# An FFN between pieces: where weight copies stand in the queues, which engine makes low parts and square sums, and where a scale chain keeps its temporary

## The chip, the cores and the metric

One core of one Trainium2 chip. The metric is the device time of one execution in microseconds. Below, PE is TensorE, DVE is VectorE, ACT is ScalarE, POOL is GpSimd, and SP is SyncE, which issues all of the kernel's loads and stores.

## The reference

One step of a hybrid streaming layer in float32: attention heads and gated linear attention heads side by side, their outputs concatenated, then a feed-forward network (FFN). 2048 prompt tokens and 32 sample tokens, model width 1024, FFN width 4096. The change touches only the end of it:

```python
h = x + concat(A, B) @ w_out
y = h + relu(rmsnorm(h) @ w_up)^2 @ w_down
```

## The kernel before

The attention and the linear attention run first (to about 745 us) and leave their concatenated output, the mix, in DRAM. Then `ffn_phase` (L1005) does the rest in three pieces, of two groups of tokens each: 320 columns per group in piece 0, 360 in pieces 1 and 2. Tokens lie along the columns, features along the partitions, in 8 blocks of 128 (KB = 8, H = 4).

Every float32 matrix is kept as a pair of a high part (a rounding copy in fp32r, made by ACT) and a low part (the difference, made by DVE or POOL), and a product is three matmuls: high by high, low by high, high by low.

A piece has these stages. `load_mix` (L955) brings the mix of a group and splits it: ACT copies the high part, DVE subtracts for the low part (L967, L968). `project_out` (L971) multiplies by w_out, giving PSUM tiles `op`, one for each feature block f. `first_group` and `second_group` (L1148, L1153) add the residual, keep y, add up the squares of y for the norm (`square`, L1134) and form the operands of a Strassen-like 2x2 scheme for the up projection: B11 and B21 from the first group, T1, T2 and T4 from combinations of both groups (`diff` L1140, `fused` L1145, `pair` L1118), then T3 and B22 after the loop. Block by block of 256 FFN columns (NF = 16), `up_head`, `up_first` (block 0) and `up_rest` do 7 products of 12 matmuls each (A11, A12, S1, S2, A22, S3, S4 by B11, B21, T1, T2, T4, T3, B22), `finished` (L1199) applies the scale, relu and square and splits u, and `down` (L1241) does 48 matmuls for each group and adds to y.

In block 0 alone `token_sums` (L1052) sums the squares over partitions with matmuls (`ss`), and a chain of 11 small DVE instructions (`rsqrt`, L163: two on the bit pattern, then three rounds of three) makes the scale, which `token_scale` (L1065) spreads with matmuls (`rb`) and ACT copies to `cb`. The order of PE in block 0: A11, A12, S1, S2, ss, A22, S3, rb, S4, down.

Weights: `up_weights` (L1074) loads a block of w_up in two halves and makes its seven operands; 7 high parts on ACT (L1088), 7 low parts (L1089) and 4 combinations (L1091) on POOL. `rows_pair` (L213) with `split_weight` (L185) does the same for w_down, two loads, two ACT copies (L194) and two POOL subtractions (L198) of 1024 columns; `load_wout` (L951) for w_out. Staging tiles come from a pool of 5 that the mix, the temporaries and the weights share; the split weights from a pool of 8. PSUM has a pool of 3 and one of 5 slots.

Two kinds of seam lie between pieces. At an up seam (the last `op` tiles, T2, T4, T3, B22, the scale, block 0) block 0's weights are split, and block 1's after them: L1185 calls `weights` for block 0 in the loop over `op` tiles, when the second group's f = 3 is done; L1283 calls it for block 1 behind `up_first`. At a mix seam (block 15 of one piece, then the next piece's projection) L1285 to L1287 split the next mix and half of w_out.

The order of the work in each engine's queue is not the program's order. A planner simulates the queues at build time and lists each engine's instructions; an instruction on one engine can be tied behind another of the same engine by an edge that costs no semaphore (as PE's are, L89). Each queue then runs strictly in that order. What the change's lines do is quoted in the diff; the central calls before are:

```python
weights = lambda pi, b: (up_weights(b, f"wu{pi}_{b}"), self.rows_pair(w_dn, 2 * b, f"wd{pi}_{b}", engs))
...
if (gi, f) == (1, H - 1):
    with tc.issue_after(self.y_loads if pi == 0 else self.last_load):
        ws[0] = weights(pi, 0)
```

Of the kernel before, what the change touches and what calls it, by code (L numbers as in the profile page):

```python
# [28 lines left out]
class Builder:  # L29
# [155 lines left out]
    def split_weight(self, src, hi, lo, hi_eng="act", lo_eng="pool", parts=1):  # L185
# [14 lines left out]
    def cols_pair(self, w, c0, name, engs=(("act", "pool"), ("act", "pool")), k0=0, nk=KB):  # L200
# [3 lines left out]
        for i in range(2):  # L204
            ks = slice(i * nk // 2, (i + 1) * nk // 2)
            self.split_weight(w[:, k0 + ks.start : k0 + ks.stop, c0 : c0 + n], h[:, ks, :], l[:, ks, :], *engs[i])
        return h, l

    def wide_pairs(self, w, c0, name, engs=(("act", "pool"), ("act", "pool")), parts=range(2)):

        return [self.cols_pair(w, c0, f"{name}{j}", engs, 4 * j, 4) for j in parts]
# [793 lines left out]
    def ffn_phase(self, pieces):  # L1005
# [7 lines left out]
        with ExitStack() as ctx:  # L1013
# [29 lines left out]

            def next_mix(pi, gi):
# [376 lines left out]
```

## Time and profile before

| | us |
|---|---|
| median of 3 runs (2358.19 to 2358.8) | 2358.7 |
| profiled execution, device time | 2357.7 |
| its span, first to last instruction | 2355.9 |
| PE busy | 2271.3 |
| DVE busy | 1452.7 |
| POOL busy | 1163.2 |
| ACT busy | 953.4 |
| mean granted TensorE clock | 0.970 |

The device time of the profiled execution is 1.8 us more than its span. The page gives for each engine the time that its instructions ran; a view of waits tells who let an engine go on after an idle time; a table by stretches gives busy times and the granted clock of any stretch, where 1.00 is 2.4 GHz and 0.50 is 1.2 GHz; a view in order of time shows single instructions. Matmuls are pipelined, so the time of one overlaps the next.

### The profile page before, as it was taken

The page shows a single profiled execution, that of the slowest core. Times are in us where ns is not written, and L with a number is a line of the kernel's source. Part 1 is how long each engine was busy: PE and PEld are TensorE (multiplying, and loading weights), DVE is VectorE, ACT ScalarE, POOL GpSimd, SP SyncE. Part 2 cuts the span into 40 slices and gives each one's busy share as a digit, 9 for nine tenths or more (in the row PEclk, how much of TensorE's full clock was granted, in tenths as well). Part 3 has the DMA queues.
Part 4 walks back from the last instruction along what each step waited for, and adds up shares of the span by engine and source line. Part 5 has one row for each costly group of instructions (what it writes and reads, how often), then busy time and mean ns, then how long its engine had stood idle before and what let it go on. Part 6 is the DMA issues. An engine that isn't in the chain of part 4 may idle for free.

```text
span 2355.9 us, 39800 instructions
## 1 busy us (share of the span) xinstructions
PE 2271.3 (96%) x15389; PEld 2130.4 (90%) x15389; DVE 1452.7 (62%) x3670; ACT 953.4 (40%) x1953; POOL 1163.2 (49%) x956
## 2 busy tenths in 40 slices
PE   6999999899998899999999899999999999999999
PEld 5777776788877899999999899999999999999999
DVE  6765656788886855555554755555555755555555
ACT  3554445454552733333334433333334533333331
POOL 3221224232430567667753466666653546666662
PEclk8999999889988899999999999999999999999999
DMA  8764563322333412222235222222227122222221
GB/s 219 148 127 101 130 166 121 84 75 74 92 93 86 119 57 91 89 72 72 81 112 169 72 72 72 72 72 72 72 62 224 37 80 72 72 72 72 72 63 51
DMA packets 214461, 221.56 MB, mean 94 GB/s; under 512 B 38736, under 2 KB 178976, under 8 KB 214272
## 3 DMA queue, kind: packets, MB, share of 16 engines
q1 hardware_dynamic: 214272, 219.02, 33.2%
q8 instruction: 121, 1.98, 0.4%
q14 instruction: 68, 0.56, 0.1%
HBM read 180.08 MB, written 38.91 MB: 93 GB/s over the span
## 4 chain that ended last, share of the span: by engine, by line
PE 79%; DVE 12%; DMA 3%; ACT 2%; POOL 2%; issue 1%; SPq 0%; DVEq 0%; POOLq 0%; ACTq 0%
PE dn L105 31%; PE op L105 7%; PE PS4B L105 4%; PE PA11B L105 4%; PE PA12B L105 4%; PE PS2T L105 4%; PE PS1T L105 3%; PE PS3T L105 3%; PE PA22T L105 3%; PE zq L105 3%; PE zr L105 3%; DVE AT L881 2%; PE zkv L105 2%; PE zv L105 2%; PE O L105 1%
## 5 line engine op out<-in xcount | busy, mean ns | idle before, releaser
L1089 POOL TENSOR_TENSOR wu<-stage,wu 128x512 fp32r<-128x512 f32 x336 | 435.2, 1304 | 528.1 <-ACT wu L1088 528.0
L1256 DVE TENSOR_TENSOR y<-y,dn 128x360 f32<-128x360 f32 (+1 forms) x768 | 392.4, 514 | 222.2 <-PE dn L105 218.7
L1088 ACT ACTIVATE wu<-stage 128x512 fp32r<-128x512 f32 x336 | 205.9, 627 | 488.8 <-PE dn L105 224.7
L1091 POOL TENSOR_TENSOR stage<-stage 128x512 f32<-128x512 f32 x192 | 250.5, 1305 | 7.5
L1209 ACT ACTIVATE r<-PA11B 128x360 f32<-128x360 f32 (+1 forms) x48 | 22.0, 458 | 317.7 <-PE PA11B L105 317.7
L1196 DVE TENSOR_TENSOR PA12B<-PA12B,r 128x360 f32<-128x360 f32 (+1 forms) x48 | 25.3, 527 | 150.2 <-PE PA12B L105 150.2
L105 PE MATMUL PS2T<-T2h,wu 128*128 128x360 f32 (+1 forms) x384 | 100.6, 324 | 13.3 <-ACT T2h L1121 13.3
L708 POOL TENSOR_TENSOR g<-g,ggla 128x512 f32<-128x512 f32 (+1 forms) x17 | 25.1, 1494 | 171.9 <-ACT g L113 171.9
L105 PE MATMUL PA22T<-T4h,wu 128*128 128x360 f32 (+1 forms) x384 | 103.1, 332 | 0.0
L105 PE MATMUL PS3T<-T3h,wu 128*128 128x360 f32 (+1 forms) x384 | 100.7, 326 | 0.0
L105 PE MATMUL PS4B<-B22h,wu 128*128 128x360 f32 (+1 forms) x384 | 100.4, 325 | 0.0
L105 PE MATMUL PS1T<-T1h,wu 128*128 128x360 f32 (+1 forms) x384 | 98.9, 321 | 0.0
L105 PE MATMUL PA11B<-B11h,wu 128*128 128x360 f32 (+1 forms) x384 | 98.8, 321 | 0.0
L105 PE MATMUL PA12B<-B21h,wu 128*128 128x360 f32 (+1 forms) x384 | 98.7, 321 | 0.0
L881 DVE COPY_PREDICATED AT<-masks,A 64x64 f32<-64x64 int32 (+1 forms) x330 | 82.9, 253 | 13.9 <-PE A L105 4.0
L105 PEld LDWEIGHTS PS2T<-T2h,wu 128*128 128x128 f32 x384 | 68.8, 190 | 14.1 <-ACT T2h L1121 14.1
L805 POOL TENSOR_TENSOR E<-cc 128x256 f32<-128x256 f32 (+1 forms) x117 | 68.2, 617 | 24.9 <-PE A L105 19.7
L497 ACT ACTIVATE P<-S,negm 128x192 f32<-128x192 f32 (+2 forms) x128 | 51.5, 417 | 52.9 <-DVE negm L492 32.8
L105 PEld LDWEIGHTS PA22T<-T4h,wu 128*128 128x128 f32 x384 | 71.4, 197 | 0.0
L105 PEld LDWEIGHTS PS3T<-T3h,wu 128*128 128x128 f32 x384 | 69.9, 193 | 0.0
L105 PEld LDWEIGHTS PS4B<-B22h,wu 128*128 128x128 f32 x384 | 69.1, 191 | 0.0
L105 PEld LDWEIGHTS PS1T<-T1h,wu 128*128 128x128 f32 x384 | 68.1, 188 | 0.0
(1006 smaller groups left out, 7769.3 us busy)
## 6 DMA issues: line engine op xcount, KB each, us to landing
stage<-in_w_up SPq DMA_DIRECT2D x96, 512.0 KB, 3.8
stage<-in_w_down SPq DMA_DIRECT2D x96, 512.0 KB, 3.9
stage<-in_w_out SPq DMA_DIRECT2D x24, 512.0 KB, 4.7
xT1a<-in_xT_prompt SPq DMA_DIRECT2D x16, 512.0 KB, 8.0
stage<-in_w_in SPq DMA_DIRECT2D x16, 512.0 KB, 5.0
x1a<-in_x_prompt SPq DMA_DIRECT2D x16, 512.0 KB, 7.2
out_yT_prompt<-y SPq DMA_DIRECT2D x32, 180.0 KB, 3.8
m<-mixT SPq DMA_DIRECT2D x11, 512.0 KB, 4.7
```

The source lines that it names most:

```text
L105: self._pe(self.T.matmul(out, lhsT, rhs, start=start, stop=stop), ns)
L497: S.activation(Pt[:, u, :n], sp[:, jp], AF.Exp, bias=negm[:, ch, u : u + 1], scale=0.125, accum_out=rsum[:, ch, u : u + 1],)
L708: G.tensor_tensor(out=gv, in0=gv, in1=ggla[:r].unsqueeze(1).broadcast_to([r, 4, P]), op=ALU.mult)
L805: G.tensor_tensor(out=e4, in0=c4, in1=ref, op=ALU.subtract)
L881: V.copy_predicated(dst, mk.unsqueeze(1).broadcast_to([L // nh, 2, w // m, m]), src[r].rearrange("s p (n m) -> s p n m", m=m),)
L1088: S.activation(h, src, AF.Copy)
L1089: G.tensor_tensor(out=l, in0=src, in1=f32(h), op=ALU.subtract)
L1091: tt = lambda o, x, y, op: G.tensor_tensor(out=o, in0=x, in1=y, op=op)
L1196: tt = lambda out, x, y, op=ALU.add: V.tensor_tensor(out=out, in0=x, in1=y, op=op)
L1209: S.activation(r0, product(b, "A11", "B11"), AF.Copy)
L1256: V.tensor_tensor(out=yg[:, f, :], in0=yg[:, f, :], in1=ps, op=ALU.add)
```

## The change

- `rsqrt` can keep its temporary q in PSUM, and does for the scale of the FFN; its first instruction now writes q instead of y.
- Copies that split weights can be tied behind a given instruction of ACT (`after`). Tied are: block 0's down weights behind T4's last high copy, and their call moves from the middle of the loop over `op` tiles to its end; block 1's up and down weights behind T3's last high copy; the next piece's first half of w_out behind the last block's high copy of u number 3.
- The low parts of the next mix are made by POOL instead of DVE.
- For the second group's f = 4, 5 and 6 the squares go to r0 and r1 in SBUF instead of back to the PSUM tile, and POOL adds them to the sum.

```diff
+    def after(self, ins, other):
+        if other is not None:
+            self.tc.add_manual_dep(ins.ins, other.ins.name, NOSYNC, reason="order")
+        return ins
...
-    def rsqrt(self, ms, r, n, name, y=None, q=None):
+    def rsqrt(self, ms, r, n, name, psum=False):
         V = self.V
-        if y is None:
-            y = self.small.tile([P, 16], F32, tag="rsq_y", name=f"rsq_y_{name}")[:r, :n]
+        y = self.small.tile([P, 16], F32, tag="rsq_y", name=f"rsq_y_{name}")[:r, :n]
+        if psum:
+            q = self.ps_s(f"rsq_q_{name}")[:r, :n]
+        else:
             q = self.small.tile([P, 16], F32, tag="rsq_q", name=f"rsq_q_{name}")[:r, :n]
-        yi = y.bitcast(I32)
-        V.tensor_scalar(out=yi, in0=ms.bitcast(I32), scalar1=1, scalar2=None, op0=ALU.logical_shift_right)
-        V.tensor_scalar(out=yi, in0=yi, scalar1=-1, scalar2=0x5F3759DF, op0=ALU.mult, op1=ALU.add)
+        yi, qi = y.bitcast(I32), q.bitcast(I32)
+        V.tensor_scalar(out=qi, in0=ms.bitcast(I32), scalar1=1, scalar2=None, op0=ALU.logical_shift_right)
+        V.tensor_scalar(out=yi, in0=qi, scalar1=-1, scalar2=0x5F3759DF, op0=ALU.mult, op1=ALU.add)
         for _ in range(3):
             V.tensor_tensor(out=q, in0=y, in1=y, op=ALU.mult)
...
             if hi_eng == "act":
-                self.S.activation(hi[:, ks], raw, AF.Copy)
+                self.after(self.S.activation(hi[:, ks], raw, AF.Copy), after)
...
-    def load_mix(self, g, hi, lo):
+    def load_mix(self, g, hi, lo, eng=None):
...
-                self.V.tensor_tensor(out=l[:, :, ts], in0=m[:, ks], in1=h[:, :, ts].bitcast(F32), op=ALU.subtract)
+                (eng or self.V).tensor_tensor(out=l[:, :, ts], in0=m[:, ks], in1=h[:, :, ts].bitcast(F32), op=ALU.subtract)
...
             def next_mix(pi, gi):
-                self.load_mix(pieces[pi][gi], hi, lo)
+                self.load_mix(pieces[pi][gi], hi, lo, G)
...
             def token_sums(name, N, accs):
-                return self.rsqrt(ms, r, 2 * n, f"y{name}")
+                return self.rsqrt(ms, r, 2 * n, f"y{name}", psum=True)
...
                 def square(gi, f, sq):
                     acc, yf = sums[gi], y[gi][:, f, :]
+                    pool = gi == 1 and H <= f < KB - 1
+                    if pool:
+                        sq = r[f % 2]
                     S.activation(sq if f else acc, yf, AF.Square)
                     if f:
-                        V.tensor_tensor(out=acc, in0=acc, in1=sq, op=ALU.add)
+                        (G if pool else V).tensor_tensor(out=acc, in0=acc, in1=sq, op=ALU.add)
...
                         fused(y[0][:, f, :], g(f), ps, ALU.subtract)
-                        pair("T4", k, ps)
+                        end[0], _ = pair("T4", k, ps)
...
                     if (gi, f) == (1, H - 1):
                         with tc.issue_after(self.y_loads if pi == 0 else self.last_load):
-                            ws[0] = weights(pi, 0)
+                            wu = up_weights(0, f"wu{pi}_0")
+                with tc.issue_after(self.y_loads if pi == 0 else self.last_load):
+                    ws[0] = wu, down_weights(pi, 0, end[0])
...
-                    S.activation(uh[i], ps, AF.Copy)
+                    hi = S.activation(uh[i], ps, AF.Copy)
+                    if i == 3:
+                        end[0] = hi
...
-                    pair("T3", k, t)
+                    end[0], _ = pair("T3", k, t)
...
-                        ws[b + 1] = weights(pi, b + 1)
+                        x = end[0] if b == 0 else None
+                        ws[b + 1] = up_weights(b + 1, f"wu{pi}_{b + 1}", x), down_weights(pi, b + 1, x)
...
-                        wo = self.load_wout(pi + 1, (0,))
+                        wo = self.load_wout(pi + 1, (0,), after=end[0])
```

## Rows read from the trace of the kernel before

**Rows 1.** The page, parts 1 and 4: busy time of each engine, and the chain that ended last by engine.

```profile
PE 2271.3 (96%) x15389; PEld 2130.4 (90%) x15389; DVE 1452.7 (62%) x3670; ACT 953.4 (40%) x1953; POOL 1163.2 (49%) x956
...
PE 79%; DVE 12%; DMA 3%; ACT 2%; POOL 2%; issue 1%; SPq 0%; DVEq 0%; POOLq 0%; ACTq 0%
```

**Rows 2.** Waits of PE over the whole span: who waited for whom, us in total, times, the longest.

```profile
PE PS2T L105 <- ACT T2h L1121: 13.3, 3, 5.4
PE dn L105 <- DVE ul L1196: 6.9, 5, 3.4
...
PE rb L105 <- DVE rsq_y_y L175: 4.6, 3, 1.9
...
PE PS2T L105 <- DVE T2l L1123: 4.3, 3, 2.7
```

**Rows 3.** Busy time in eight stretches: length, busy us and instructions of PE, PEld, DVE, ACT and POOL, granted clock, DMA share, GB/s. The first three run from the first product of block 0 to the first of block 1 (up seams of pieces 0, 1 and 2), the next two from the end of the last block's products to the next piece's first output projection (mix seams 1 and 2); then one regular block of 320 and one of 360 columns; last, four microseconds within mix seam 1.

```profile
792.53:834.70 42.17, 31.69 (x167) 30.44 (x165) 33.46 (x58) 19.40 (x42) 26.42 (x17) 0.72 0.37 113
1308.35:1344.76 36.41, 29.23 (x157) 27.72 (x157) 32.52 (x56) 19.00 (x39) 24.20 (x15) 0.86 0.36 116
1862.89:1899.29 36.40, 29.92 (x157) 28.45 (x157) 32.51 (x56) 19.00 (x39) 24.29 (x15) 0.86 0.38 116
1224.26:1244.99 20.73, 16.78 (x98) 15.76 (x97) 17.54 (x35) 7.76 (x17) 5.78 (x3) 0.92 0.63 198
1781.73:1799.54 17.81, 16.17 (x97) 15.71 (x97) 16.36 (x33) 8.94 (x14) 7.21 (x4) 1.00 0.95 319
880.70:907.14 26.44, 26.44 (x182) 26.44 (x182) 14.42 (x31) 9.44 (x19) 18.67 (x14) 1.00 0.26 81
1425.97:1455.63 29.66, 29.66 (x182) 29.66 (x181) 15.83 (x31) 9.79 (x19) 18.66 (x14) 1.00 0.23 71
1229.00:1233.00 4.00, 3.98 (x16) 3.99 (x17) 2.23 (x5) 1.98 (x3) 2.38 (x1) 0.57 0.79 241
```

**Rows 4.** PE in up seam 1, in order of time: start, us, what; in brackets the idle time before it and its releaser.

```profile
1319.89 0.67 PE L105 MATMUL PS2T<-T2h,wu 128*128 128x360 f32 x1 [3.96 <-ACT T2h L1121]
1321.29 0.67 PE L105 MATMUL PS2T<-T2l,wu 128*128 128x360 f32 x1 [0.73 <-DVE T2l L1123]
...
1322.05 2.42 PE L105 MATMUL ss<-ones,sums 128*120 128x1 f32 x12
...
1332.26 1.60 PE L105 MATMUL rb<-packed,rsq_y_y 120*128 120x120 f32 x12 [1.86 <-DVE rsq_y_y L175]
...
1336.90 0.43 PE L105 MATMUL dn<-ul,wd_0h 128*128 128x360 f32 x1 [0.57 <-DVE ul L1196]
```

**Rows 5.** VectorE in up seam 1, in order of time (x2 is two in a row).

```profile
1310.69 3.85 DVE L1125 SCALAR_TENSOR_TENSOR B22l<-y,packed,B22h 128x360 fp32r<-128x360 f32 x2
...
1315.91 1.41 DVE L1143 SCALAR_TENSOR_TENSOR r<-y,packed,r 128x360 f32<-128x360 f32 x1
...
1317.68 1.15 DVE L1125 SCALAR_TENSOR_TENSOR B22l<-y,packed,B22h 128x360 fp32r<-128x360 f32 x1
1318.75 0.58 DVE L1146 SCALAR_TENSOR_TENSOR op<-y,packed,op 128x360 f32<-128x360 f32 x1
...
1324.51 0.16 DVE L1062 TENSOR_SCALAR msy<-ss 120x6 f32<-120x6 f32 x1
...
1327.02 1.19 DVE L173 TENSOR_TENSOR rsq_q_y<-rsq_y_y 120x6 f32<-120x6 f32 x1
...
1331.09 1.11 DVE L175 SCALAR_TENSOR_TENSOR rsq_y_y<-rsq_q_y,rsq_y_y 120x6 f32<-120x6 f32 x1
```

**Rows 6.** Groups of VectorE instructions over the whole span: busy us, mean ns of one.

```profile
L1256 DVE TENSOR_TENSOR y<-y,dn 128x360 f32<-128x360 f32 x512 | 269.0, 528 | 155.3 <-PE dn L105 153.0 <-DMA stage<-in_w_down 0.5
...
L1125 DVE SCALAR_TENSOR_TENSOR B22l<-y,packed,B22h 128x360 fp32r<-128x360 f32 x8 | 11.8, 1499 | 0.7 <-ACT B22h L1121 0.7
...
L1125 DVE SCALAR_TENSOR_TENSOR B21l<-op,packed,B21h 128x360 fp32r<-128x360 f32 x8 | 4.7, 593 | 9.8 <-ACT B21h L1121 9.8
...
L968 DVE TENSOR_TENSOR T4l<-m,T4h 128x512 fp32r<-128x512 f32 x4 | 2.6, 678 | 0.0
```

**Rows 7.** GpSimd in up seam 1, in order of time.

```profile
1307.53 5.07 POOL L198 TENSOR_TENSOR wd_0l<-stage,wd_0h 128x1024 fp32r<-128x1024 f32 x2 [15.63 <-ACT wd_0h L194]
```

**Rows 8.** The page, part 5: the costliest group, GpSimd's low halves of the up weights.

```profile
L1089 POOL TENSOR_TENSOR wu<-stage,wu 128x512 fp32r<-128x512 f32 x336 | 435.2, 1304 | 528.1 <-ACT wu L1088 528.0
```

**Rows 9.** VectorE in up seam 0, in order of time.

```profile
797.86 4.54 DVE L1125 SCALAR_TENSOR_TENSOR B22l<-y,packed,B22h 128x320 fp32r<-128x320 f32 x3
```

**Rows 10.** Mix seam 1, all engines in order of time.

```profile
1222.67 1.67 ACT L967 ACTIVATE T4h<-m 128x128 fp32r<-128x128 f32 x4
...
1222.84 2.40 POOL L198 TENSOR_TENSOR wo_00l<-stage,wo_00h 128x1024 fp32r<-128x1024 f32 x1 [4.84 <-ACT wo_00h L194]
...
1223.00 2.40 DVE L968 TENSOR_TENSOR T4l<-m,T4h 128x128 fp32r<-128x128 f32 x1 [1.03 <-ACT T4h L967]
...
1224.24 0.42 ACT L1203 ACTIVATE PA22T<-PA22T 128x320 f32<-128x320 f32 x1
...
1228.49 0.47 DVE L1196 TENSOR_TENSOR ul<-PA22T,uh 128x320 fp32r<-128x320 f32 x1
...
1229.02 0.41 PE L105 MATMUL dn<-ul,wd_15h 128*128 128x320 f32 x1 [3.42 <-DVE ul L1196]
```

**Rows 11.** PE in mix seam 2.

```profile
1784.69 0.43 PE L105 MATMUL dn<-ul,wd_15h 128*128 128x360 f32 x1 [1.64 <-DVE ul L1196]
```

More of the change, by code (lines that the diff above doesn't have):

```diff
@@ L183, in rms, with split_weight @@
         return self.rsqrt(ss, r, 1, name)
-    def split_weight(self, src, hi, lo, hi_eng="act", lo_eng="pool", parts=1):
+    def split_weight(self, src, hi, lo, hi_eng="act", lo_eng="pool", parts=1, after=None):
         k, c = src.shape[1], src.shape[2]
@@ L205, in cols_pair, with wide_pairs, rows_pair @@
             ks = slice(i * nk // 2, (i + 1) * nk // 2)
-            self.split_weight(w[:, k0 + ks.start : k0 + ks.stop, c0 : c0 + n], h[:, ks, :], l[:, ks, :], *engs[i])
+            self.split_weight(w[:, k0 + ks.start : k0 + ks.stop, c0 : c0 + n], h[:, ks, :], l[:, ks, :], *engs[i], after=after)
         return h, l
-    def wide_pairs(self, w, c0, name, engs=(("act", "pool"), ("act", "pool")), parts=range(2)):
-        return [self.cols_pair(w, c0, f"{name}{j}", engs, 4 * j, 4) for j in parts]
-    def rows_pair(self, w, k0, name, engs=(("act", "pool"), ("act", "pool"))):
+    def wide_pairs(self, w, c0, name, engs=(("act", "pool"), ("act", "pool")), parts=range(2), after=None):
+        return [self.cols_pair(w, c0, f"{name}{j}", engs, 4 * j, 4, after) for j in parts]
+    def rows_pair(self, w, k0, name, engs=(("act", "pool"), ("act", "pool")), after=None):
         h, l = self.w_tile(f"{name}h"), self.w_tile(f"{name}l")
@@ L217, in rows_pair @@
         for i in range(2):
-            self.split_weight(w[:, k0 + i : k0 + i + 1, :], h[:, i : i + 1], l[:, i : i + 1], *engs[i])
+            self.split_weight(w[:, k0 + i : k0 + i + 1, :], h[:, i : i + 1], l[:, i : i + 1], *engs[i], after=after)
         return h, l
@@ L948, in gla_phase, with load_wout @@
                         Q.dma_start(self.o[name][2 * p + hh], St[key][hh * 64 : hh * 64 + 64, p, :])
-    def load_wout(self, pi, halves=range(2), engs=(("act", "pool"), ("act", "pool"))):
+    def load_wout(self, pi, halves=range(2), engs=(("act", "pool"), ("act", "pool")), after=None):
         w_out = self.a["w_out"].rearrange("(k p) n -> p k n", p=P)
-        return [self.wide_pairs(w_out, 512 * fh, f"wo{pi}_{fh}", engs) for fh in halves]
-    def load_mix(self, g, hi, lo):
+        return [self.wide_pairs(w_out, 512 * fh, f"wo{pi}_{fh}", engs, after=after) for fh in halves]
+    def load_mix(self, g, hi, lo, eng=None):
         off = 0
@@ L1042, in load_y @@
                 return yt
+            end = [None]
             def next_mix(pi, gi):
@@ L1072, in token_scale, with up_weights @@
                 S.activation(cb[gi], rb, AF.Copy)
-            def up_weights(b, name):
+            def up_weights(b, name, after=None):
                 raw = []
@@ L1087, in pair @@
                     h, l = ws[x]
-                    S.activation(h, src, AF.Copy)
+                    self.after(S.activation(h, src, AF.Copy), after)
                     G.tensor_tensor(out=l, in0=src, in1=f32(h), op=ALU.subtract)
@@ L1105, in ffn_phase @@
             engs = (("act", "pool"), ("act", "pool"))
-            weights = lambda pi, b: (up_weights(b, f"wu{pi}_{b}"), self.rows_pair(w_dn, 2 * b, f"wd{pi}_{b}", engs))
+            down_weights = lambda pi, b, after=None: self.rows_pair(w_dn, 2 * b, f"wd{pi}_{b}", engs, after)
             mix = list(self.mix)
```

14 lines of the change are left out of this document (8 added, 6 removed).

## The prediction, made before the changed kernel ran

> **What bounds the kernel now.** I read the page first. PE is busy for 96% of the span and carries 79% of the chain that ended last [rows 1], so only time that PE does not use, or uses at the lower clock, can be won. The waits of PE say where it is: its four largest waits add up to 29.1 us, and all four lie in the FFN, at the seams between pieces [rows 2]. The table by stretches prices a seam. A regular block takes 26.44 us at 320 columns and 29.66 us at 360, PE never idle, for 180 matmuls (7 products of 12, two groups of 48 down matmuls) [rows 3]. An up seam holds 132 of them, so 19.39 or 21.75 us, and the sums and broadcasts of the scale. Those two show 2.42 us at half clock and 1.60 [rows 4]; halving the first, I allow 2.8 us (an estimate). The seams take 42.17, 36.41 and 36.40 us [rows 3]: they lose 20.0, 11.9 and 11.9. A mix seam holds 96 down matmuls, 14.1 or 15.8 us; they take 20.73 and 17.81 [rows 3]: lost 6.6 and 2.0. Together 52.4 us, which is all that this change can touch.
>
> Why they lose it. In up seam 1 PE waits 3.96 us for the last high part of T2, 0.73 us for its low part, 1.86 us for the scale chain and 0.57 us for u [rows 4], and runs much of the rest at 1.2 GHz: granted clock 0.86 over the seam, 0.72 in seam 0 [rows 3]. The operands are late because VectorE is: the combination that the last T2 is copied from starts at 1318.75, behind B22's low parts, of which two take 3.85 us and one 1.15, and a difference that takes 1.41 [rows 5]. The groups say what is odd about them: B22l, two SBUF tensors in, takes 1.50 us in the mean; B21l, the same instruction with one input from PSUM, 0.59 [rows 6]. GpSimd's low parts of the down weights run just then, 5.07 us for two [rows 7]. In seam 0 three B22l take 4.54 us [rows 9]. The scale chain shows the same: 0.16 us for the instruction that reads PSUM, 1.19 and 1.11 for two on SBUF alone, 7.7 us from 1324.51 to the end of the last [rows 5]. An instruction with a PSUM input is not held: 512 of them take 528 ns in the mean beside a GpSimd that is busy 63% of a regular block [rows 3, 6].
>
> **The change, part by part.**
>
> *Copies of the down weights behind T4's last copy, of block 1's weights behind T3's.* This takes the 5.07 us of GpSimd and block 1's 1.30 us pieces [rows 7, 8] out of the stretch before the last T2. Four B22l give back 0.9 us each and the difference 0.8: 4.4 us. ACT does no more than before. Down weights are due at the first down matmul, at least three products and the scale's 2.8 us after T4's last copy, some 9 us, against 2 us of copies and 5 of low parts. Block 1's need 11 GpSimd instructions, 14.3 us by rows 8, and they start behind those 5: some 20 us after T4, while its first two pairs are due after about 18 and only the rest after 28. The first pairs come first, so hidden; were the cover gone, each us late is a us of PE. The two SP loads of down weights move past no other load, but hold two of the five staging tiles longer, so the second half of block 1's up weights lands some 9 us later, inside the same slack.
>
> *Three sums of squares to GpSimd.* VectorE loses three instructions of 0.5 us, about one of them ahead of the last T2: 0.5. GpSimd gains three of about 0.92 us (1304 ns x 360/512, rows 8), each of which can hold one two-SBUF instruction of VectorE: 0 to 2.8 us, of which I take 1. ACT writes the squares to r0 and r1; the first product's copy and T3's first difference then wait for GpSimd to have read them, which they need only after a product's 2 us. The last sum, still on VectorE, waits for GpSimd's third; GpSimd has little else there. First stretch: waits of 4.69 less 4.9 plus 1, so 0.8 us left.
>
> *The chain in PSUM.* Of eleven instructions eight now have one tensor input at most in SBUF and a PSUM operand beside or behind it. The three squarings of y still read SBUF twice, with a PSUM output that no row shows. Bounds: 0.17 each, or held by a whole GpSimd instruction, 1.3 to 2.5 us. I take held for 1.25 us each, because the same line was held in rows 5 and its inputs have not moved: 3.8. With twelve steps of 0.2 us and one T3 instruction between them the chain takes 6.7 us instead of 7.7, since the moved weights now lie beside it. At full clock PE has two products, 4.0 us, to cover it: 2.7 us of wait remain. T3's last difference and low part meet the same GpSimd work, and T3's last copy can stand behind 2 us of moved copies on ACT: 0 to 5 us, I take 1.5. The wait for u, 0.6, stays. The temporary takes one of five PSUM slots; the last projection's and PS2T's are free by then, so I cost it at nothing (a product's 2 us if not).
>
> *Clock.* The 3.42 us stall in mix seam 1 was followed by four us at 0.57 [rows 3, 10], a loss of 1.7; the 1.64 us stall of mix seam 2 by none, the stretch shows 1.00 [rows 3, 11]. The waits left lie between, so 0 or 1.7 per up seam; I take 1.7.
>
> Up seams therefore keep 0.8 + 2.7 + 1.5 + 0.6 + 1.7 = 7.3 us each: gains of 12.7, 4.6 and 4.6 (bounds 6 to 17, 0 to 9 and 0 to 9).
>
> *The mix.* In mix seam 1 u's second part is late because ACT copies T4 four times (1.67 us) ahead of the square that leads to it (1224.24), and VectorE's T4l waits 2.40 us behind a GpSimd instruction of the same length that began 0.16 us before it; the low part of u starts at 1228.49, and PE has waited 3.42 us [rows 10]. With the low parts gone from VectorE and the output weights' copies behind u's last, this chain follows its products directly. I leave 0.6 us: gains of 6.0 (3.5 to 6.6) and 1.8 (0 to 2.0). What GpSimd takes on: 2880 columns per group at 1304 ns per 512 [rows 8], 7.5 us where VectorE took 0.68 per 512 [rows 6], and 4 x 2.40 for the output weights. From the last product on T2, four products before 1224.26 and so about 1217, that ends near 1236 (the last T4 and u's copies let it start in pieces); the projection, 96 matmuls after 1224.26, needs it at 1238.8. Loads of the mix come later where a staging tile waits for GpSimd; they lie in the same slack.
>
> The Trainium skill speaks against both moves: Perfetto Trace Analysis, section Optimizing Scalar/DVE Operations, says that GpSimd and VectorE share an SBUF read port, so that moving work between the two might not help. By that the 7.8 us of the mix would be 0 and the sum 21.9; rows 6 and 10 limit it here, since VectorE's other work in that seam has a PSUM operand and was not held.
>
> Sum: 12.7 + 4.6 + 4.6 + 6.0 + 1.8 = 29.7 us. The profiled execution took 2357.7 us (span 2355.9), so 2328.0; the median lies 1.0 above it: **2329**, by its own bounds 2319 to 2339.
>
> **The rivals.**
>
> *The hold is moved, not removed.* T3's differences and low parts, B22's rest and the squarings all meet the moved weights, and the three sums hold B22l as before. For it: GpSimd's work is not less; against it: T2, which PE needs first, comes free of it. Up seams 1 and 2 then gain nothing, seam 0 its lower bound of 6, the mix 7.8: 13.8, so **2345**. The Trainium skill, SBUF — State Buffer, section Who interferes with whom, has this rule: two SBUF inputs contend with a GpSimd instruction that reads SBUF, as an exclusive lock, wherever the output goes. Rows 5 and 6 agree for outputs in SBUF; by it the squarings are held as I took them.
>
> *All but small waits go.* GpSimd happens to idle beside T3 and the chain, and the clock never falls; each up seam keeps 3 us: 17 + 8.9 + 8.9 + 7.8 = 42.6, so **2316**. For it: nearly all excess of rows 5 comes from one cause.
>
> *GpSimd becomes the bound of the mix seams (slower).* If its queue holds the mix's low parts behind output weights that wait for u, the projection waits. The slack is 2.8 us; beyond it each us costs PE one at each of two seams, and 1.7 of clock. The up seams' 21.9 are used up when it is late by 9.2 us; at 13 us late the time is **2366**. For it: GpSimd takes twice VectorE's time per column; against it: it idled 4.84 us ahead of one weight in rows 10 alone.
>
> *It does not do what it says.* The order in each queue is planned at build with costs of its own, which no row shows; a new order may put other work before the last T2, and the stalls stay in size: **2358**, within 4.
>
> **How the numbers follow.** Forecast 0.47, hold moved 0.25, all gone 0.13, no change 0.08, slower 0.07. 0.2% is 4.7 us, about what a measurement of this kernel can tell from no change. Faster by more: 0.47 + 0.25 + 0.13 = 0.85; same 0.08; slower 0.07. The range takes in the forecast's bounds, the moved hold and the case in which all goes, each with a few us: 2313 to 2349.
>
> **What would show it.** In the up seams the last T2 wait of PE under 1 us in each; B22l near 0.6 us; eight of the chain's steps at 0.2 us and the squarings longer; the wait for the broadcast still there. In mix seam 1 no stall in the first down group and no T2l or T4l on VectorE. Granted clock over the up seams above 0.95. It is wrong if PE's first wait at an up seam is still several us, or if PE waits for a low part of the mix or of weights that GpSimd made.

## The result, and the profile after

The changed kernel takes 2324.66 us in the median of 4 runs (2323.11 to 2326.91), the kernel before beside it 2358.44 (2356.5 to 2358.8): a ratio of 0.9859, 95% interval 0.9842 to 0.9876. The forecast was 2329 in 2313 to 2349, so 1.4% faster against 1.26% forecast. The profiled execution took 2323.38 us with a span of 2321.6, 34.3 less than before.

The page, parts 1 and 4, of the kernel after, which answer to [rows 1]:

```profile
PE 2256.5 (97%) x15389; PEld 2117.4 (91%) x15389; DVE 1410.5 (61%) x3631; ACT 952.7 (41%) x1953; POOL 1197.3 (52%) x995
...
PE 75%; DVE 11%; DMA 5%; POOL 3%; ACT 3%; issue 2%; SPq 1%; DVEq 0%; POOLq 0%; ACTq 0%
```

VectorE lost 42 us of busy time and GpSimd gained 34; PE is 15 us less busy because less of its work ran at the lower clock. The stretches of the seams after, cut at the same instructions and with the same columns as [rows 3] (up seam 0, mix seam 1, up seam 1, mix seam 2, up seam 2):

```profile
791.45:820.52 29.07, 27.00 (x167) 25.57 (x165) 25.74 (x56) 16.89 (x38) 14.96 (x12) 0.88 0.28 91
1210.90:1225.01 14.11, 14.11 (x98) 14.11 (x97) 8.97 (x20) 7.25 (x12) 13.10 (x10) 1.00 0.92 263
1288.37:1319.83 31.46, 28.57 (x157) 27.49 (x157) 26.82 (x58) 17.08 (x36) 12.41 (x9) 0.89 0.21 68
1756.80:1773.61 16.81, 16.36 (x97) 15.81 (x97) 9.79 (x20) 8.84 (x14) 15.25 (x11) 1.00 0.99 324
1836.97:1864.98 28.01, 25.28 (x157) 24.29 (x157) 24.60 (x53) 15.36 (x33) 11.85 (x8) 1.00 0.23 76
```

Against [rows 3] the seams are shorter by 13.10, 6.62, 4.95, 1.00 and 8.39 us. Two small terms lie beside them: the first product of block 0 starts 1.08 us sooner (791.45 for 792.53), and the stretch from block 1 of piece 0 to mix seam 1 is 0.82 longer (390.38 for 389.56). Together 34.3, the whole difference.

The waits of PE over the whole span, which answer to [rows 2]; the 13.3 us for T2's high part and 6.9 for u's low part are 0.4 and 0.6 now, and these two are the largest left in the FFN:

```profile
PE PS2T L111 <- DVE T2l L1134: 3.5, 2, 1.8
...
PE rb L111 <- DVE rsq_y_y L183: 2.1, 1, 2.1
```

PE at the points of [rows 4], in up seam 1 and then in up seam 2 of the kernel after:

```profile
1296.37 0.43 PE L111 MATMUL PS2T<-T2h,wu 128*128 128x360 f32 x1 [0.41 <-ACT T2h L1132]
1298.63 0.43 PE L111 MATMUL PS2T<-T2l,wu 128*128 128x360 f32 x1 [1.83 <-DVE T2l L1134]
...
1299.06 2.23 PE L111 MATMUL ss<-ones,sums 128*120 128x1 f32 x12
...
1307.41 1.49 PE L111 MATMUL rb<-packed,rsq_y_y 120*128 120x120 f32 x12
...
1311.39 0.43 PE L111 MATMUL dn<-uh,wd_0h 128*128 128x360 f32 x1 [0.52 <-ACT uh L1222]
...
1845.04 1.32 PE L111 MATMUL ss<-ones,sums 128*120 128x1 f32 x12
...
1852.51 1.57 PE L111 MATMUL rb<-packed,rsq_y_y 120*128 120x120 f32 x12 [2.10 <-DVE rsq_y_y L183]
...
1857.11 0.43 PE L111 MATMUL dn<-ul,wd_0h 128*128 128x360 f32 x1 [0.63 <-DVE ul L1214]
```

The 3.96 us for T2's high part are 0.41 in seam 1 and nothing in seam 2, but 1.83 for the low part are left in seam 1. There the granted clock then falls to 1.2 GHz (`ss` takes 2.23 us, in seam 2 1.32), and with two products at the lower clock the chain is hidden; in seam 2 the clock stays at 1.00 and PE waits 2.10 us for the chain.

VectorE's B22 low parts of 360 columns after, the group that answers to [rows 6]; the three of up seam 0, which answer to [rows 9], with the GpSimd instructions beside them; and the chain in up seam 2 with the GpSimd instructions beside it:

```profile
L1136 DVE SCALAR_TENSOR_TENSOR B22l<-y,packed,B22h 128x360 fp32r<-128x360 f32 x8 | 4.7, 613 | 0.2 <-ACT B22h L1132 0.2
...
793.03 3.37 DVE L1136 SCALAR_TENSOR_TENSOR B22l<-y,packed,B22h 128x320 fp32r<-128x320 f32 x3
...
792.99 3.06 POOL L1153 TENSOR_TENSOR sums<-sums,r 128x320 f32<-128x320 f32 x3
...
1846.92 0.17 DVE L178 TENSOR_SCALAR rsq_q_y<-msy 120x6 int32<-120x6 int32 x1
1847.12 0.16 DVE L179 TENSOR_SCALAR rsq_y_y<-rsq_q_y 120x6 int32<-120x6 int32 x1
1847.32 1.69 DVE L181 TENSOR_TENSOR rsq_q_y<-rsq_y_y 120x6 f32<-120x6 f32 x1
...
1849.45 1.89 DVE L181 TENSOR_TENSOR rsq_q_y<-rsq_y_y 120x6 f32<-120x6 f32 x1
...
1851.78 0.17 DVE L181 TENSOR_TENSOR rsq_q_y<-rsq_y_y 120x6 f32<-120x6 f32 x1
...
1846.58 4.72 POOL L206 TENSOR_TENSOR wd_0l<-stage,wd_0h 128x1024 fp32r<-128x1024 f32 x2 [10.12 <-ACT wd_0h L202]
```

B22's low parts of 360 columns fell from 1499 to 613 ns. The three of up seam 0 fell less, from 4.54 to 3.37 us: they run beside the three sums that moved to GpSimd. Below, a hold is the time by which a VectorE instruction lasts longer beside a GpSimd instruction than it does alone. In the chain two squarings, with two SBUF inputs and an output in PSUM, are held; they end at 1849.01 and 1851.34; the two GpSimd instructions end at about 1848.9 and 1851.3. The third squaring, with GpSimd idle, takes 0.17.

### The profile page after: what moved, and what is told of

It reads as the page before. It is cut to its first block, busy times and chain, and to the rows that moved or that the text cites. A ratio compares the mean times of both kernels' runs of the same rounds, so it can differ in the third digit from the quotient of the medians.

```text
span 2321.6 us, 39805 instructions
## 1 busy us (share of the span) xinstructions
PE 2256.5 (97%) x15389; PEld 2117.4 (91%) x15389; DVE 1410.5 (61%) x3631; ACT 952.7 (41%) x1953; POOL 1197.3 (52%) x995
## 4 chain that ended last, share of the span: by engine, by line
PE 75%; DVE 11%; DMA 5%; POOL 3%; ACT 3%; issue 2%; SPq 1%; DVEq 0%; POOLq 0%; ACTq 0%
PE dn L111 31%; PE PA22T L111 4%; PE PS3T L111 4%; PE PS2T L111 4%; PE PS4B L111 4%; PE PS1T L111 4%; PE PA11B L111 4%; PE PA12B L111 4%; PE zq L111 3%; PE op L111 3%; PE zr L111 3%; DVE AT L889 2%; PE zkv L111 2%; PE zv L111 2%; PE O L111 1%
```

## The experiments

Every kernel was also profiled, and its seams were cut at the same instructions. Lengths in us; "rest" runs from PE's last wait for the linear attention's state (739.42 after) to the end of the span. The part ahead of that point took 737.1 to 748.0 us in kernels that differ behind it, so the medians carry some microseconds that are not the edit's, and the seams decide. Ratios are to the kernel before on the same chip.

| | median | ratio, 95% interval | up 0 | mix 1 | up 1 | mix 2 | up 2 | rest |
|---|---|---|---|---|---|---|---|---|
| before | 2358.4 | 1 | 42.17 | 20.73 | 36.41 | 17.81 | 36.40 | 1616.1 |
| after | 2324.7 | 0.9859, 0.9842 to 0.9876 | 29.07 | 14.11 | 31.46 | 16.81 | 28.01 | 1582.2 |
| e1 mix's low parts on VectorE | 2328.8 | 0.9871, 0.9856 to 0.9886 | 29.01 | 16.21 | 29.84 | 17.43 | 28.02 | 1582.9 |
| e2 q in SBUF | 2329.5 | 0.9870, 0.9851 to 0.9890 | 29.48 | 14.12 | 30.30 | 16.97 | 28.72 | 1581.8 |
| e3 sums on VectorE | 2330.7 | 0.9876, 0.9862 to 0.9889 | 31.27 | 14.12 | 28.79 | 16.33 | 28.82 | 1582.0 |
| e4 no ties at the up seams | 2356.8 | 0.9989, 0.9978 to 0.9999 | 41.86 | 14.12 | 38.44 | 16.91 | 37.99 | 1612.0 |
| e5 x ahead of the up weights | 2327.4 | 0.9865, 0.9852 to 0.9879 | 29.12 | 14.12 | 30.43 | 17.36 | 28.02 | 1581.3 |
| e6 whole chain in PSUM | 2324.0 | 0.9846, 0.9831 to 0.9861 | 31.71 | 15.00 | 28.64 | 16.31 | 25.68 | 1577.7 |
| e7 e5 and e6 | 2323.1 | 0.9848, 0.9831 to 0.9865 | 28.82 | 14.43 | 28.85 | 16.15 | 25.70 | 1575.2 |
| e8 e4 with zeros for low halves | 2338.5 | 0.9906, 0.9891 to 0.9921 | 31.40 | 14.12 | 33.88 | 16.93 | 34.22 | 1591.9 |
| e9 stores, then x, then w_out | 2323.2 | 0.9847, 0.9830 to 0.9863 | 29.13 | 14.12 | 28.96 | 16.30 | 28.01 | 1579.1 |
| e10 e9 and e6 | 2322.5 | 0.9835, 0.9821 to 0.9850 | 28.89 | 14.12 | 28.27 | 16.57 | 25.69 | 1575.9 |
| e11 mix's low parts twice | 2335.9 | 0.9889, 0.9870 to 0.9908 | 29.12 | 14.12 | 29.59 | 15.82 | 29.57 | 1592.3 |

**e4: the ties at the up seams undone.**

```diff
-                            wu = up_weights(0, f"wu{pi}_0")
-                with tc.issue_after(self.y_loads if pi == 0 else self.last_load):
-                    ws[0] = wu, down_weights(pi, 0, end[0])
+                            ws[0] = up_weights(0, f"wu{pi}_0"), down_weights(pi, 0)
...
-                        x = end[0] if b == 0 else None
+                        x = None
```

> The changed kernel without the ties at the up seams: block 0's down weights are called for in the middle of the loop again, and neither they nor block 1's weights wait for T4's or T3's last copy. The mix, the sums and the chain stay as changed. Theory (the up seams' gain is the weight copies and the GpSimd work behind them, out of the way of the last T2): PE's wait for the last T2 is 3 to 6 us again in each up seam, B22's low parts near 1.5 us, and 18 to 24 us of the 25.7 are given back: 2343 to 2349. Rival (the planner's new order, the sums and the chain made most of it): under 10 us slower, below 2335.

The up seams gave back 12.8, 7.0 and 10.0 us, 29.8 in all and more than the theory's 18 to 24, and the kernel is 0.1% from the one before. So the ties are worth more than the 26.4 us that the up seams gained; without them the other edits do little there, and seams 1 and 2 are 2.0 and 1.6 us longer than before. In up seam 0 the waits are not the old ones: PE waits 4.2 us for T2 (8.1 before) and 4.1 for the square sums (none before).

**e8: is it GpSimd's reading, or the copies' place on ScalarE?** e4, with the low halves of block 0's down weights and of block 1's weights left out: GpSimd writes zeros.

```diff
+            if after == 0:
+                self.G.memset(lo[:, ks].bitcast(F32), 0.0)
+                continue
             eng.tensor_tensor(out=lo[:, ks], in0=raw, in1=hi[:, ks].bitcast(F32), op=ALU.subtract)
...
-                    G.tensor_tensor(out=l, in0=src, in1=f32(h), op=ALU.subtract)
+                    if after == 0:
+                        G.memset(f32(l), 0.0)
+                    else:
+                        G.tensor_tensor(out=l, in0=src, in1=f32(h), op=ALU.subtract)
```

> The kernel of e4 (no ties at the up seams), and with the low halves of block 0's down weights and of block 1's up and down weights left out: GpSimd writes zeros in their place, so it reads nothing; the copies on ScalarE stand where they stood. The four combinations of the up weights on GpSimd stay. Theory (VectorE's two-SBUF instructions wait for GpSimd instructions that read SBUF): B22's low parts fall from 1.5 us to 0.6, and the up seams of 41.9, 38.4 and 38.0 us fall by 3 to 7 us each. Rival (the copies ahead of T2's last high part on ScalarE are the cost): the seams stay within 2 us, PE's wait for T2's high part stays near 3 us. Second rival (any GpSimd work holds VectorE, writes too): B22's low parts stay at 1 us or more.

Against e4 the seams fall by 10.5, 4.6 and 3.8 us, with ScalarE's copies where they were. That is what GpSimd's low halves cost; in up seam 0 PE's wait for the sums, 0.9 us instead of 4.1, is part of it. B22's low parts fall to a mean of 0.93 us at 360 columns (1.81 in e4) and 1.07 at 320 (1.47), not to the theory's 0.6. What still lies between e8 and the changed kernel, 2.3, 2.4 and 6.2 us, is left for the copies' place and for the four combinations that GpSimd still reads; no run parts these two. In up seam 1 three held VectorE instructions (1.59, 1.15 and 1.60 us), beside these combinations, stand closely ahead of the last T2's low part, and PE waits 3.6 us for it.

A piece of zeros also takes GpSimd 0.49 us where a subtraction took 1.30, so the seams alone do not tell whether GpSimd's reading counts or only its time. Single instructions do. VectorE and GpSimd in up seam 0 of e8, in order of time, show both kinds of GpSimd work side by side:

```profile
803.56 1.55 DVE L1164 SCALAR_TENSOR_TENSOR r<-y,packed,r 128x320 f32<-128x320 f32 x1
805.03 0.48 DVE L1140 TENSOR_TENSOR T2l<-op,T2h 128x320 fp32r<-128x320 f32 x1
...
805.89 1.52 DVE L1164 SCALAR_TENSOR_TENSOR r<-y,packed,r 128x320 f32<-128x320 f32 x1
807.33 0.48 DVE L1140 TENSOR_TENSOR T3l<-r,T3h 128x320 fp32r<-128x320 f32 x1
...
803.24 1.52 POOL L1108 TENSOR_TENSOR stage<-stage 128x512 f32<-128x512 f32 x1
...
805.79 1.27 POOL L1108 TENSOR_TENSOR stage<-stage 128x512 f32<-128x512 f32 x1
807.01 0.98 POOL L1104 MEMSET wu<- 128x512 f32 x2
```

Two differences with two SBUF inputs, begun while GpSimd combines two tensors, take 1.55 and 1.52 us (0.54 when GpSimd is idle, at 811.48); T2l, with one input in PSUM, 0.48 beside GpSimd's sum at 804.73. T3l has two SBUF inputs again, begins while GpSimd writes zeros, and takes 0.48; beside a combination in up seam 1 the same line took 1.60. The Trainium skill, SBUF — State Buffer, section Who interferes with whom, states just this: two SBUF inputs contend with a GpSimd instruction that reads SBUF, not with one that only writes it. The trace agrees on both halves.

**e2: q back in SBUF.** `psum=True` in `token_sums` is taken away.

> The changed kernel, with the temporary q of the scale chain back in SBUF. Theory (an instruction with two SBUF operands waits for GpSimd, one with a PSUM operand does not): the chain goes from 5.0 and 5.6 us back to 7 to 8, several steps near 1 us again while the low parts of the down weights run, and PE waits about 2 us longer for the broadcast in up seam 2; in seams 0 and 1 half clock hides some of it. 2 to 5 us slower, 2327 to 2330. Rival (the squarings carry all of the hold, wherever q lies): the chain keeps its length within 0.5 us and the time stays within 1 us of 2324.7.

The theory's size is missed. VectorE and GpSimd in up seam 2 of e2:

```profile
1843.49 2.08 DVE L178 TENSOR_SCALAR rsq_q_y<-msy 120x6 int32<-120x6 int32 x1
1845.61 2.29 DVE L179 TENSOR_SCALAR rsq_y_y<-rsq_q_y 120x6 int32<-120x6 int32 x1
1847.93 0.17 DVE L181 TENSOR_TENSOR rsq_q_y<-rsq_y_y 120x6 f32<-120x6 f32 x1
...
1843.14 4.72 POOL L206 TENSOR_TENSOR wd_0l<-stage,wd_0h 128x1024 fp32r<-128x1024 f32 x2 [10.13 <-ACT wd_0h L202]
```

The first two steps are held now, and the nine behind them are free. There are two holds because there are two GpSimd instructions: whatever steps come first sit them out, and the chain ends 1.8 us behind GpSimd (6.4 us long, where q in PSUM gave 5.6). Moving q alone moved the holds to the squarings; it gained 0.7 us in seam 2 and 0.4 in seam 0. In seam 1 e2 is even shorter, because its wait at T2 was 1.5 us and the clock stayed at 1.00; PE waits 2.8 us for the chain instead.

**e6: no step of the chain with two SBUF inputs.** The mean square stays in PSUM as well, and the product is taken in another order.

```diff
-            V.tensor_tensor(out=q, in0=y, in1=y, op=ALU.mult)
-            V.scalar_tensor_tensor(out=q, in0=q, scalar=-0.5, in1=ms, op0=ALU.mult, op1=ALU.mult)
+            V.tensor_tensor(out=q, in0=y, in1=ms if psum else y, op=ALU.mult)
+            V.scalar_tensor_tensor(out=q, in0=q, scalar=-0.5, in1=y if psum else ms, op0=ALU.mult, op1=ALU.mult)
...
-                ms = self.small.tile([P, 8], F32, tag="msy", name=f"msy_{name}", bufs=1)[:r, : 2 * n]
-                V.tensor_scalar(out=ms, in0=ps, scalar1=1.0 / D, scalar2=EPS, op0=ALU.mult, op1=ALU.add)
-                return self.rsqrt(ms, r, 2 * n, f"y{name}", psum=True)
+                V.tensor_scalar(out=ps, in0=ps, scalar1=1.0 / D, scalar2=EPS, op0=ALU.mult, op1=ALU.add)
+                return self.rsqrt(ps, r, 2 * n, f"y{name}", psum=True)
```

> The changed kernel, with the mean square kept in PSUM too and each round of the chain taken as q = y*ms, q = -0.5*q*y, y = (q+1.5)*y, so that every one of the eleven steps has a PSUM operand and none reads two tensors in SBUF. Theory (a step with two SBUF operands starts only when GpSimd's running instruction ends, two such steps per chain, and nothing else makes it long): all steps 0.15 to 0.2 us, the chain 2.3 us instead of 5.0 and 5.6, PE's wait of 2.10 us for the broadcast in up seam 2 goes, seam 2 takes about 26 us; seam 1, where no such wait is left, stays. 2 us faster, near 2322.5. Rival (PE then waits for VectorE's next sums or u instead): seam 2 above 27.5 us and the time within 1 us of 2324.7. Second rival (GpSimd holds small PSUM steps as well): the chain above 4 us.

VectorE in up seam 2 of e6, the steps at the held squarings' places and the last, and GpSimd; then the stretch:

```profile
1850.22 0.17 DVE L181 TENSOR_TENSOR rsq_q_y<-rsq_y_y,ss 120x6 f32<-120x6 f32 x1
...
1850.83 0.17 DVE L181 TENSOR_TENSOR rsq_q_y<-rsq_y_y,ss 120x6 f32<-120x6 f32 x1
...
1851.85 0.16 DVE L183 SCALAR_TENSOR_TENSOR rsq_y_y<-rsq_q_y,rsq_y_y 120x6 f32<-120x6 f32 x1
...
1849.47 4.73 POOL L206 TENSOR_TENSOR wd_0l<-stage,wd_0h 128x1024 fp32r<-128x1024 f32 x2 [10.13 <-ACT wd_0h L202]
...
1839.86:1865.54 25.68, 25.03 (x157) 24.31 (x157) 21.48 (x53) 14.86 (x32) 11.35 (x8) 1.00 0.25 83
```

All steps lie inside GpSimd's 4.73 us and none is held: 2.4 us for the chain, and seam 2 is 2.3 us shorter, as the theory had it. Seam 1 fell too (28.64), which it did not foresee. Seam 0 became 2.6 us longer, though its queues stand in the order of e7, where it takes 28.82. In both PE waits 1.7 us for T2. In e7 half clock follows at once (0.50 from 802.6 to 806.3); in e6 it comes later, PE waits 1.4 us more for T3's high part, and the clock falls a second time (0.56 from 815 to 821).

**e1: the mix's low parts on VectorE.** `next_mix` calls `load_mix` without `G`.

> The changed kernel, with the low parts of the next mix back on VectorE; the output weights' copies stay tied behind the last block's third u. Theory (the low parts on VectorE are what made u late in the mix seams): mix seam 1 goes from 14.1 us back towards 18 to 20 and mix seam 2 from 16.8 to 17.5, so 4 to 7 us slower than the changed kernel's 2324.7, some 2329 to 2332. Rival (it was the output weights' copies on ScalarE and GpSimd, and the hold of 2.4 us that they put on two T4 low parts): these are still tied, so no more than 1 us slower, 2325 to 2326, and mix seam 1 below 15 us.

Between the two: 2.1 us of 6.6 in mix seam 1 and 0.6 of 1.0 in mix seam 2 are given back. The rest is left for the output weights' copies behind u, which no run undid by themselves. And the place is another than I had named. VectorE and then PE in mix seam 1 of e1:

```profile
1219.41 2.24 DVE L976 TENSOR_TENSOR T3l<-m,T3h 128x224 fp32r<-128x224 f32 x1
1221.57 2.58 DVE L976 TENSOR_TENSOR B22l<-m,B22h 128x224 fp32r<-128x224 f32 x1
1224.07 0.87 DVE L1276 TENSOR_TENSOR y<-y,dn 128x320 f32<-128x320 f32 x2
...
1224.60 0.41 PE L111 MATMUL dn<-uh,wd_15h 128*128 128x320 f32 x1 [0.91 <-DVE y L1276]
```

u came in time. Two low parts of the second group, held for 2.24 and 2.58 us beside the output weights on GpSimd, kept VectorE from adding to y, and PE waited for a PSUM slot.

**e3: the sums on VectorE.** `pool = False` in `square`.

> The changed kernel, with the three square sums back on VectorE. Theory (VectorE is late at the last T2 and three instructions of 0.53 us more make it later): the waits for the last T2 low part grow by 0.5 to 1.5 us in up seams 0 and 1, nothing in seam 2, where VectorE is not behind: 1 to 3 us slower, 2326 to 2328. Rival (the sums on GpSimd hold VectorE's B22 as much as they free it): within 0.5 us of 2324.7 or up to 1 us faster.

Neither: seam 0 is 2.2 us longer (waits of 1.1 us at T2 and 1.7 for T3's high part, with a second fall of the clock as in e6) and seam 2 is 0.8 longer, seam 1 2.7 shorter (no wait at T2 there, one of 2.0 us for T3's high part at clock 1.00), and the rest of the kernel takes 1582.0 for 1582.2. On the whole the three sums moved nothing; the planner's new order of the queues moved the waits about. One effect of the sums on GpSimd does show. The three B22 low parts of up seam 0, without GpSimd's sums beside them, in e3:

```profile
802.96 1.47 DVE L1136 SCALAR_TENSOR_TENSOR B22l<-y,packed,B22h 128x320 fp32r<-128x320 f32 x3
```

In the changed kernel they take 3.37 us, so the sums hold them for 1.9.

**e5 and e9: why up seam 1 gains less than seam 2.** The seams' queues hold the same work in the same order, but VectorE takes the last `op` tile 3.02 us after its products in seam 1 and 0.36 after in seam 2. In piece 1 VectorE waits for the second group's x until 30.6 us after the projection's start, in piece 2 until 21.1 us. e5 queues the up weights' loads behind x's:

```diff
-                        with tc.issue_after(self.y_loads if pi == 0 else self.last_load):
+                        with tc.issue_after(self.y_loads):
                             wu = up_weights(0, f"wu{pi}_0")
```

> The changed kernel with one edit: in pieces 1 and 2 the loads of block 0's up weights queue on SP behind the loads of the second group's x, not ahead of them. Theory (up seam 1 gains less than seam 2 because these x loads land 17.7 us after the first group's, held up in SP's queue behind an up-weight load that waits for a staging tile, and VectorE is still 2.7 us behind when the last op tile comes): the second group's first residual in piece 1 moves up by 5 us or more, PE's two waits at T2 in up seam 1 (0.41 and 1.83 us) go, its granted clock is 1.00 and the seam takes 28.0 to 28.5 us instead of 31.46: 3 us faster, near 2321.5. Rival (VectorE's backlog in seam 1 is its own work, not the late load): seam 1 within 0.5 us of 31.46 and the time within 1 us of 2324.7.

x came only 1.4 us sooner. SP's queue in e5, 1210 to 1265 us, by releaser:

```profile
SPq L1048 <- DMA out_yT_prompt<-y: 6.0, 1, 6.0
```

The load writes where the last piece's y lay, whose stores stood behind w_out's loads. e9 puts the stores first:

```diff
                         next_y = load_y(pi + 1, 0)
-                        wo += self.load_wout(pi + 1, (1,))
                     down(b, 1)
                 if pi + 1 < len(pieces):
                     y = [next_y, load_y(pi + 1, 1)]
+                    with tc.issue_after(self.y_loads):
+                        wo += self.load_wout(pi + 1, (1,))
```

> The changed kernel with one edit at the mix seams: on SP the stores of a piece's last second group go ahead of the second half of w_out's loads, and these go behind the second group's x loads. e5 moved these x loads past the up weights alone, and they then waited 6.0 us for those stores. Theory (VectorE's backlog, which makes the last T2 late in up seam 1, comes from x landing 29 to 31 us after the projection's start; in piece 2 it is 21 us): in piece 1 the second group's first residual comes 6 to 12 us sooner, VectorE takes the last op tile less than 0.5 us late, as in seam 2, PE has no wait at T2 in up seam 1 and the seam takes 28.0 to 28.5 us instead of 31.46; in all 3 us faster than 2324.7. Rival (the late x costs nothing, VectorE's work in that stretch is simply too long): VectorE takes the last op tile 2.5 us late as before, seam 1 stays at 30 to 31.5 us. Second rival (the later w_out takes over): PE waits in the projection for w_out's second half.

| | first residual with x after | VectorE late by | waits at T2 | up seam |
|---|---|---|---|---|
| after | 30.6 | 3.02 | 0.41 + 1.83 | 31.46 |
| e5 | 29.2 | 2.00 | 1.5 | 30.43 |
| e9 | 25.9 | 1.33 | 0.8 | 28.96 |
| seam 2 after | 21.1 | 0.36 | 0 | 28.01 |
| seam 1, e3 | 28.5 | 0.29 | 0 | 28.79 |

From the changed kernel to e5 and e9 the four go down together, so the late x is a part of the backlog. It is not enough by itself: in e3, whose queues have another order, x is nearly as late as in e5 and VectorE takes the last `op` tile 0.29 us after its products (the projection runs from 1235.75 to 1299.11):

```profile
1264.28 0.98 DVE L1142 TENSOR_TENSOR op<-op,y 128x360 f32<-128x360 f32 x2 [6.52 <-DMA y<-in_xT_prompt]
...
1299.40 0.53 DVE L1142 TENSOR_TENSOR op<-op,y 128x360 f32<-128x360 f32 x1
```

And what is left in e9 is not x's alone. ScalarE and VectorE ahead of the first residual, which follows at 1253.47:

```profile
1251.56 1.06 ACT L202 ACTIVATE wo_10h<-stage 128x1024 fp32r<-128x1024 f32 x1 [4.22 <-DMA stage<-in_w_out]
1252.53 0.46 ACT L1151 ACTIVATE op<-y 128x360 f32<-128x360 f32 x1
...
1253.02 0.53 DVE L1153 TENSOR_TENSOR sums<-sums,op 128x360 f32<-128x360 f32 x1 [5.05 <-ACT op L1151]
```

VectorE idles 5.05 us for a square that stands on ScalarE behind a copy of w_out, and the copy waits 4.22 us for its load, which e9 had moved back. So the second rival came in part, on ScalarE; PE itself never waits for w_out.

**e7 and e10: the edits joined.**

> The two edits of e5 and e6 together. Theory: with no wait at T2 and none for the broadcast, up seams 1 and 2 both take about 26 us, 5.5 and 2 us less than in the changed kernel, so 7 us faster, near 2317.5. Rival (the two do not add, since half clock in seam 1 hid the chain, or a wait for u takes their place): 3 to 4 us faster.

> The edit of e9 and the chain of e6 together. Theory: up seams 1 and 2 both take 25.7 us, as seam 2 did in e6 and e7; with seam 0 at 29 us that is 5.8 and 2.3 us less than in the changed kernel: near 2316.5 and faster than both kernels by more than 0.2%. Rival (half clock after a wait elsewhere, or a new wait for u): seam 1 at 28 us or more, 3 to 4 us faster in all.

Seam 2 came as expected in both (25.70, 25.69), seam 1 did not (28.85, 28.27): T2's low part is still waited for, 1.5 and 0.9 us, and the clock over the seam is 0.94. The rest is 7.0 and 6.3 us shorter than in the changed kernel. e10 has the lowest ratio of all, 0.9835, but its interval overlaps the changed kernel's; faster than before it is for certain, faster than the changed kernel by its seams.

**e11: how thin is GpSimd's cover in the mix seams?** Each low part of the next mix is made twice.

```diff
-                (eng or self.V).tensor_tensor(out=l[:, :, ts], in0=m[:, ks], in1=h[:, :, ts].bitcast(F32), op=ALU.subtract)
+                for _ in range(2 if eng else 1):
+                    (eng or self.V).tensor_tensor(out=l[:, :, ts], in0=m[:, ks], in1=h[:, :, ts].bitcast(F32), op=ALU.subtract)
```

> The changed kernel, in which GpSimd makes each low part of the next mix twice. Theory (GpSimd's work in the mix seams is hidden, with about 2.5 us to spare in mix seam 1: its last output weight ends at 1222.5, the projection starts at 1225.0): 7 us more ahead of the output weights' low parts and 6 us more ahead of the second group's projection give waits of 0.5 to 4 us at seam 1 and 0 to 2 us at seam 2, for low parts that GpSimd made: 2 to 5 us slower. Rival (GpSimd is far from the bound there): no wait of PE behind GpSimd in the projections and within 1 us of 2324.7. Second rival (GpSimd is the bound already): 7 us or more at each seam, 14 us slower.

More than I gave it: 10.1 us. The mix seams stay, the projections behind them go from 63.36 to 72.42 and 64.80. PE's waits in piece 1's projection, and the one that is longest with the instructions that it waits for:

```profile
PE op L111 <- POOL T3l L977: 4.5, 1, 4.5
PE op L111 <- POOL wo_01l L206: 2.4, 2, 1.3
...
1254.83 0.44 PE L111 MATMUL op<-T3l,wo_00h 128*128 128x360 f32 x1 [4.45 <-POOL T3l L977]
...
1251.88 2.35 POOL L206 TENSOR_TENSOR wo_10l<-stage,wo_10h 128x1024 fp32r<-128x1024 f32 x1 [0.83 <-ACT wo_10h L202]
1254.19 0.58 POOL L977 TENSOR_TENSOR T3l<-m,T3h 128x192 fp32r<-128x192 f32 x1
```

The waits sum to 6.9 of the 9.1 us. In the changed kernel the second group's low parts end at 1229.84 and PE wants them at 1225.01 + 4 x 3.96 = 1240.85; 13 us more use that up, and an output weight that the new order put ahead of the last T3l did the rest. This is the mechanism of the prediction's slower rival, reached with twice the work. Where the prediction gave 2.8 us of slack to all of it, the changed kernel has 2.5 us ahead of the projection's start (the last output weight ends at 1222.48) and 11.0 us ahead of the second group.

## Why the prediction was right, and where its sizes were off

**The mechanism held.** The sum was 29.7, the profile shows 34.3. The combinations behind T2 were late through the hold; e4 and e8 show it. Several sizes were off, and in up seams 0 and 1 it is luck that their sum came out.

**Up seam 0**: 12.7 forecast, 13.1 measured. 1.69 us are left at T2 (0.8 forecast), none at the chain (2.7 forecast), 0.2 at T3 (1.5 forecast), and the lower clock, 0.88 over 29.07 us, costs about 3.5 us (an estimate; 1.7 forecast). The errors nearly cancel.

**Up seam 1**: 4.6 forecast, 4.95 measured, again with other parts: 2.24 us at T2 instead of 0.8, none at the chain and at T3, and again about 3.5 us of clock instead of 1.7 (an estimate, from 0.89 over 31.46 us).

**Up seam 2**: 4.6 forecast, 8.4 measured. This is the step that failed: "Up seams therefore keep 0.8 + 2.7 + 1.5 + 0.6 + 1.7 = 7.3 us each". One sum stood for three seams. Seam 2 kept 2.10 + 0.63; the 0.8 at T2, the 1.5 at T3 and the 1.7 of clock were all zero. The sum also charged every seam with both a wait for the chain, worked out "At full clock", and a loss at half clock. In the changed kernel a seam has one or the other: in seams 0 and 1 the clock fell and PE did not wait for the chain, in seam 2 the clock stayed and PE waited 2.10 us. And "0 or 1.7 per up seam" was no bound: the estimates are 3.5, 3.5 and 0. What makes seams 1 and 2 differ is in part how late x comes (e5, e9), which [rows 2 to 5] do not show and I did not look up; e3 shows that the order of the queues counts too, and how the two share it stays open.

**The chain**: 6.7 us forecast, 5.0 and 5.6 measured in seams 1 and 2. The term "held for 1.25 us each" counted three squarings; two were held (1.07 or 1.69, and 1.89), one for each GpSimd instruction; in seam 0 T3's last low part took the second hold (2.52 us). I priced the wrong thing: the number of holds is GpSimd's, not the chain's, and so q's move by itself was worth 0.7 us in seam 2 (e2). What would have taken the holds away is e6.

**The sums**: 0.5 forecast, less 1 of hold. The hold is 1.9 us in up seam 0, about as long as the wait that is left at T2 there; as a sum nothing is shown (e3).

**The mix**: 6.0 and 1.8 forecast, 6.62 and 1.00 measured. In seam 2 0.32 us of a wait for u are left. The path was the wrong one in part: e1, which keeps the output weights' ties, shows that low parts on VectorE then hold back y, not u.

**Covers**: "Block 1's need 11 GpSimd instructions" ended, in the prediction, with "so hidden"; the cover was 0.55 us short. Block 1's first copies came at 1312.31 in piece 1, behind u's, and in piece 0 PE waits:

```profile
832.12 0.56 PE L111 MATMUL PS2T<-T2h,wu 128*128 128x320 f32 x2 [0.55 <-POOL wu L1100]
```

That is most of the 0.82 us lost behind up seam 0. It is absent in e3, e4, e6 and e8. A wait "for a low part of the mix or of weights that GpSimd made" was a sign of being wrong; it came, at this size.

**The signs named**: T2's wait under 1 us in each seam (1.69, 2.24, 0), the clock above 0.95 (0.88, 0.89, 1.00): met in seam 2 alone. B22l near 0.6: met in seams 1 and 2 (613 ns), not in seam 0 (three in 3.37 us). Eight short steps, no stall in mix seam 1's first down group and no low part of the next mix on VectorE: met. "the wait for the broadcast still there": met in seam 2 alone.

**Two slips of the working.** The waits called "its four largest waits" are the four largest of the FFN: six waits of 4.5 to 6.6 us, ahead of the FFN, lie among them in the view of [rows 2]. And the bounds of the terms add up to 9.5 to 43.6 us, so 2315 to 2349, not "2319 to 2339". Neither touches the sum.

**The page that spoke against it**: by the Trainium skill, Perfetto Trace Analysis, section Optimizing Scalar/DVE Operations, moving work between VectorE and GpSimd might not help. Here the mix seams gained 7.6 us, of which e1 gives 2.7 to the move; the sums gained nothing, and in up seam 0 they held VectorE for 1.9 us.

## What to carry to other kernels

Where a VectorE instruction has two SBUF inputs and takes two or three times its usual time, look at what GpSimd reads just then, and move one of the two in time, or put one operand in PSUM; the short chain here paid one hold for each GpSimd instruction beside it until no step was left that could be held. Price each seam by its own rows: two that ran the same queue differed here, in part through a load that landed late 30 us earlier. Do not add a wait worked out at full clock to a loss at half clock in the same seam. And when work goes to a slower engine, work out its slack at every consumer, not at the first alone.

## What was not expected of the hardware

Two steps with one SBUF input and an SBUF output, the shift and the multiply of `rsqrt` on 120x6, were held as long as those with two (2.08 and 2.29 us in e2), and were free (0.16 and 0.17) when one side lay in PSUM.

A wait of about the same length was followed by different clocks: over up seam 1 the granted clock is 0.89 after 2.24 us of waits at T2 and after 1.5 (e5), 0.94 after 1.7 (e1) and after 0.8 (e9), and 1.00 after 1.5 (e2); e6 and e7 differ by 2.9 us in seam 0 with the same order of the queues. What decides it stays open.

The part ahead of the FFN, whose PE order is the same, ends between 737.1 and 748.0 us in these kernels, and the kernel before is already 1.7 to 6.2 us ahead of the others at the instruction that it starts at 100 us; why stays open too.
